# Two gate projections of a hybrid mixer as seven products of quarters

## The chip, the cores and the metric

The kernel runs on one core of a Trainium2 chip. It has five engines that work side by side, each through its own instructions in order: TensorE (PE; its weight loads are shown as PEld), VectorE (DVE), ScalarE (ACT), GpSimd (POOL) and SyncE (SP), which mostly issues DMAs. The metric is the device time of one execution in microseconds. A run of the kernel is compared with runs of the kernel before; smaller is better.

## What is computed

One decoder layer on 512 tokens of width 1024, in float32: a SwiGLU FFN, a mixer of two recurrent head groups, and a second FFN, each inside its own pair of norms.

```python
x = x + 0.5 * rms_norm(swiglu_ffn(rms_norm(x, norm_pre[0]), ffn1_w_in, ffn1_w_out), norm_post[0])
mixed = token_mixer(rms_norm(x, norm_pre[1]), w_mix_in, conv_w, ..., w_mix_out)
x = x + rms_norm(mixed, norm_post[1])
x = x + 0.5 * rms_norm(swiglu_ffn(rms_norm(x, norm_pre[2]), ffn2_w_in, ffn2_w_out), norm_post[2])
```

The mixer projects the normed x by one matrix and cuts the result into parts. The change concerns two of them, `hgate` (HG) and `mo` (MO), of 512 columns each:

```python
hq, hf, hi, hgate, mq, mk, mv, mo, mig, mfg = split_cols(h @ w_in, SPLIT_SIZES)
...
hg_o = rms_norm(hgrn2_chunkwise(...), hg_norm) * silu(hgate)
ml_o = rms_norm(mlstm_chunkwise(...), ml_norm) * sigmoid(mo)
return concatenate([hg_o, ml_o]) @ w_out
```

## The kernel before

**Number format.** Every float32 operand of a projection is split in a high part (`hi`, rounded to fp32r) and a low part (`lo = raw - hi`). A product takes three matmuls: high by high, high by low, low by high (`mm3`, lines L187, L188, L189). For a weight, ScalarE makes the high part and VectorE the low part (`split`, L283 and L285; for `w_mix_out`, whose rows are also scaled, L288 and L291 in halves of 512). The activations are split the same way into four tiles `xq`, one for each quarter of x (256 tokens by 512 columns): `to_t` transposes on TensorE (L353), then ScalarE casts (L359) and VectorE subtracts (L360).

**Stages.** FFN 1, the mixer, FFN 2. In the FFNs most projections are already made by seven products of quarters in place of eight (matmuls of 128x256 at L608, L947 and L955). The weight sums that the second projection of an FFN needs are made in DRAM: `sums_ahead` copies quarters of the weight to a DRAM tile by three DMAs of SP and adds others to it by three accumulating DMAs of GpSimd (L887). `make_sums` issues the next DMA of up to a few of these groups; it is called at places in the program (`EVERY`, the jobs of the mixer). FFN 1 has 13 such groups, FFN 2 has 15; the copies of seven of FFN 2's groups are issued at the end of FFN 1 (`copies_early`).

**The mixer.** The program is written in one order by hand; a scheduler at build time then orders each engine's instructions and may move one ahead of others whose operands it expects later (`behind` and `issue_after` pin some). Projections are generators (`job_f`, `job_t`); the recurrences call `fill(n)` between their steps, and each call runs the front job up to its next yield, so that projections fill TensorE while VectorE, ScalarE and GpSimd work on the recurrence. `job_t` makes 512 columns for all tokens in four PSUM banks: 4 weight tiles of 256 rows, 4 token tiles, 2 halves, 3 matmuls of 128x512 each, which is 96 matmuls. The last jobs are HG and MO; HG's result goes through Silu into the left half of `y`, MO's through Sigmoid and a multiplication on VectorE (L1771) into the right half (`gate_mo`).

Around them stand, in this order: `mlstm_scores`, four steps of `mlstm_values` (on VectorE L1679 to L1690, on GpSimd L344 and L1687), four steps of `hgrn_values` (VectorE L1651, GpSimd L345, VectorE L1657), the rest of MO, the transposes of `y` (L353), and the output projection `mix_out0`/`mix_out1`, whose first half needs `y`'s high and low parts (L359, L360).

**Loads.** All weights come through one ring of SBUF tiles (`raw`) by DMAs of SP; a load is issued behind the split of an earlier item (`load_due`). x itself (`xs`, 512 x 1024) stays in SBUF from the first norm to the output.

Of the kernel before, what the change touches and what calls it, by code (L numbers as in the profile page):

```python
# [14 lines left out]
P = 128  # L15
# [15 lines left out]
HQ, HF, HI, HG, MQ, MV, MO, MG = 0, 512, 1024, 1536, 2048, 2560, 3072, 3584  # L31
LEVELS = (1, 64, 32, 16, 8, 4, 2)
# [57 lines left out]
EVERY, EARLY, AHEAD = 5, 7, 13  # L90
# [28 lines left out]
class Layer:  # L119
    def __init__(self, ctx, tc, aps):  # L120
# [12 lines left out]
        self.xs = self.cp.tile([P, NT, D], F32, name="xs")  # L133
# [12 lines left out]
        }  # L146

# [112 lines left out]
    def split(self):  # L260
# [7 lines left out]
        else:  # L268
# [4 lines left out]
            n, o = self.lie("out" if it.key[1] == "out" else "mix" if it.key[0] == "mix" and b == 512 else "any")  # L273
# [20 lines left out]
        with self.behind(*self.hold):  # L294
            for out, other in it.adds:
                o, c = self.raw[out], self.raw[other]

                late = out[1] >= (HEAD if out[0] == "f1" else 1)
                added = (nc.vector if late else nc.gpsimd).tensor_tensor(o, o, c, op=ALU.add)  # L299
                if not late:  # L300
                    self.pooled = added
# [155 lines left out]
    def root(self, i, turned=False):  # L457

        x = self.xs[:, i, :]
# [8 lines left out]
    def scaled(self, i, g, r, xn, h):  # L468
        v = slice(512 * h, 512 * h + 512)
        scaled = self.nc.vector.scalar_tensor_tensor(xn[:, v], self.xs[:, i, v], r, g[:, v], op0=ALU.mult, op1=ALU.mult)  # L470
# [12 lines left out]
    def post1(self, i, y, parts, rms, pieces, g, out=None):  # L483
# [11 lines left out]
        for h, v in (late, (0, y)) if turned else ((0, y), late):  # L495
            x = self.xs[:, i, 512 * h : 512 * h + 512]
# [79 lines left out]
    def open_ffn(self, ctx, second=False):  # L576

        self.after_next, self.c22 = None, []
        self.second, self.filled = second, FILLED2 if second else FILLED
        hp = self.hpool = ctx.enter_context(self.tc.tile_pool(name=self.nm("hp"), bufs=1))  # L580
# [207 lines left out]
    def ffn_in(self):  # L788

        nc = self.nc  # L790
        if not self.second:
            self.begun = ()
            self.sums_due("f1")
        for n, (p, t) in enumerate(ORDER2[len(HEADS2) :] if self.second else ORDER[len(HEADS) :]):
            if n > 14 and n % EVERY == 0 and not self.second:
                self.make_sums()
            if n == 14 and self.second:

                with self.behind(self.pooled):
# [75 lines left out]
    def sums_ahead(self, f, h, k2, early=False):  # L875

        nc, to = self.nc, self.sums_of[f, h, k2]
        w, last = (self.ffn1_w_out, self.ffn2_w_out)[f == "f2"][0], self.loaded1 if early else self.loaded
        q = w[k2 * 2 * P : (k2 + 1) * 2 * P, h * 512 : (h + 1) * 512].rearrange("(k p) (c f) -> p k c f", p=P, f=QUARTER)
        with self.behind(last):  # L880
            nc.sync.dma_start(to[:, 0], q[:, 0, 1])
            nc.sync.dma_start(to[:, 1], q[:, 1, 0])
            nc.sync.dma_start(to[:, 2:], q[:, 1])
        yield
        for a, b, v in ((0, 2, q[:, 0, :1].broadcast_to([P, 2, QUARTER])), (2, 3, to[:, :1]), (3, 4, to[:, 2:3])):
            with self.behind(*([self.selected] if f == "f2" else [])):
# [3 lines left out]
    def sums_due(self, f, n=None, done=0):  # L890
        self.ahead, self.making = deque([k for k in self.sums_of if k[0] == f][done:n]), []

    def copies_early(self):

        self.begun = deque(self.sums_ahead(*k, early=True) for k in [k for k in self.sums_of if k[0] == "f2"][:EARLY])
# [3 lines left out]
    def make_sums(self):  # L899

        n = min(3, len(self.begun))
# [5 lines left out]
    def ffn_out(self, gpost_row, scale, after, trans, head):  # L907
# [89 lines left out]
        if self.second:  # L997
            self.sums_due("f2", done=AHEAD)
        n = 0
        for half in range(2):  # L1000
            C = [[self.ps() for _ in range(2)] for _ in range(2)]
            M, T, left = None, None, len(QF[half])
            for m, k2 in enumerate(OF[half][: PAIRS - LF * half]):
# [20 lines left out]
                if half == 0 and n % 2:  # L1024
# [14 lines left out]
        if not self.second:  # L1039
            self.copies_early()  # L1040
# [54 lines left out]
    def job_t(self, name, then):  # L1095

        acc = [self.ps() for _ in range(NT)]
        for k2 in range(ND // 2):
            w = self.pull()
            if name in ("hi", "mv"):  # L1100
                self.make_sums()
            for i in range(NT):
# [10 lines left out]
                yield  # L1113

    def mix_items(self):
# [17 lines left out]
        f(HF), f(HQ), f(MQ), t(HI), t(MV), t(HG), t(MO)  # L1133
# [66 lines left out]
    def small_params(self):  # L1200
# [29 lines left out]
        for g in range(2):  # L1230
            nc.sync.dma_start(self.gb[32 * g : 32 * g + 4, :], bias[g].rearrange("(h o) -> h o", o=1))
# [292 lines left out]
    def conv(self, n, ps):  # L1524
# [3 lines left out]
        nc.scalar.copy(x, ps)  # L1528
        tap = lambda j: self.prm[:, 4 * j + n : 4 * j + n + 1]
# [177 lines left out]
    def mixer(self):  # L1707
        nc, tc = self.nc, self.tc
        self.got, self.jobs = set(), deque()
        self.sums_due("f2", AHEAD, EARLY)  # L1710
        with tc.tile_pool(name="ma", bufs=1) as ma:
# [7 lines left out]
            self.eend = ma.tile([P, 16], F32, name="eend")  # L1719
            with tc.tile_pool(name="mb", bufs=1) as mb:  # L1720
# [30 lines left out]
            with tc.tile_pool(name="mc", bufs=1) as mc:  # L1751
                self.y = mc.tile([P, NT, D], F32, name="y")
                self.jobs.append(self.job_t("hg", lambda i, ps: nc.scalar.activation(self.y[:, i, :W], ps, AF.Silu)))
# [147 lines left out]
```

## Time and profile before

| | us |
|---|---|
| median of three runs | 934.02 (931.58 to 934.08) |
| the profiled execution | 933.69 |
| its span in the profile | 932.0 |
| TensorE busy | 921.7 (99%) |
| VectorE busy | 765.9 (82%) |
| ScalarE busy | 525.2 (56%) |
| GpSimd busy | 186.9 (20%) |

The span runs from the first to the last instruction that the profiler shows; 1.7 us of the profiled time lie around it. Busy time is the sum over an engine's instructions, overlaps counted once. In rows of the timeline the numbers are start and duration; x4 is the count of instructions in the row, and what stands in brackets is the idle time of the engine before it and what released it. In the chain of waits the duration of a matmul is its spacing in the stream, while the timeline and the groups show it from issue to end, so that neighbours overlap. FFN 1 ends and the mixer begins between about 320 and 347 us; the mixer ends at about 600 us.

### The profile page before, as it was taken

What the parts mean: (1) busy time and instruction counts of PE and PEld (TensorE: products, weight loads), DVE (VectorE), ACT (ScalarE), POOL (GpSimd) and SP (SyncE); (2) the same over time, 40 slices, a digit from 0 to 9 for tenths busy, and PEclk for the clock granted to TensorE, in tenths of its full rate; (3) what the DMA queues carried; (4) which work ended last, traced back from release to release, by engine and by line L of the source; (5) the groups of instructions that cost most, each with busy time, mean ns of one, the idle gap of its engine ahead of it and who ended that gap; (6) DMA issues with size and microseconds to landing.
All of it is one profiled execution on the core that took longest, in us unless ns stands there. A gap on an engine that the chain in (4) does not pass through costs nothing.

```text
span 932.0 us, 18308 instructions
## 1 busy us (share of the span) xinstructions
PE 921.7 (99%) x7423; PEld 887.4 (95%) x7423; DVE 765.9 (82%) x992; ACT 525.2 (56%) x757; POOL 186.9 (20%) x256
## 2 busy tenths in 40 slices
PE   8999999999999999999999999999999999999997
PEld 7999999999999999998887888899999999999997
DVE  5899978889888776698847564799898989998886
ACT  6645455557565466956633444495454545756661
POOL 3531112121111045452321210304000000011002
PEclk9999999999999999999999999999999999999999
DMA  9245679776797925798742124452453435279542
GB/s 310 76 138 157 181 182 214 195 157 142 209 273 238 262 65 150 151 184 208 152 98 69 46 72 132 137 162 66 135 159 123 136 111 174 84 221 261 165 153 91
DMA packets 118766, 145.42 MB, mean 156 GB/s; under 512 B 7413, under 2 KB 91417, under 8 KB 118682
## 3 DMA queue, kind: packets, MB, share of 16 engines
q1 hardware_dynamic: 102714, 129.05, 44.2%
q0 software_dynamic: 15680, 14.69, 11.6%
q8 instruction: 58, 0.95, 0.4%
q10 hardware_dynamic: 288, 0.52, 0.2%
q14 instruction: 26, 0.21, 0.1%
HBM read 142.14 MB, written 31.46 MB: 186 GB/s over the span
## 4 chain that ended last, share of the span: by engine, by line
PE 62%; ACT 1%; DVE 0%; issue 0%; POOL 0%; DVEq 0%; POOLq 0%; ACTq 0%
PE ps L608 22%; PE ps L955 8%; PE ps L538 6%; PE ps L187 5%; PE ps L189 5%; PE ps L188 5%; PE ps L947 4%; PE ps L1373 2%; PE ps L353 1%; PE ps L548 1%; PE ps L1466 0%; PE ps L1671 0%; PE ps L1644 0%; PE ps L1419 0%; PE ps L1668 0%; PE ps L1431 0%
## 5 line engine op out<-in xcount | busy, mean ns | idle before, releaser
L283 ACT CAST w<-raw 128x1024 fp32r<-128x1024 f32 x246 | 251.3, 1028 | 199.0 <-PE ps L608 93.6
L285 DVE TENSOR_TENSOR w<-raw,w 128x1024 fp32r<-128x1024 f32 x246 | 298.9, 1219 | 30.9 <-ACT w L283 29.5
L608 PE MATMUL ps<-xq,w 128*128 128x256 f32 x2016 | 237.1, 277 | 0.0
L608 PEld LDWEIGHTS ps<-xq,w 128*128 128x128 f32 x2016 | 232.9, 188 | 0.0
L608 PE MATMUL ps<-sq,w 128*128 128x256 f32 x1512 | 178.0, 276 | 0.3
L608 PEld LDWEIGHTS ps<-sq,w 128*128 128x128 f32 x1512 | 174.2, 188 | 1.0 <-ACT ps L659 0.9
L299 DVE TENSOR_TENSOR raw<-raw,raw 128x1024 f32<-128x1024 f32 x72 | 89.8, 1251 | 7.8 <-DMA raw<-in_ffn_w_in_dram 6.1
L955 PE MATMUL ps<-w,hs 128*128 128x256 f32 x672 | 81.0, 276 | 0.0
L947 PE MATMUL ps<-w,hs 128*128 128x256 f32 x672 | 79.2, 276 | 0.0
L955 PEld LDWEIGHTS ps<-w,hs 128*128 128x128 f32 x672 | 78.4, 188 | 0.0
L187 PE MATMUL ps<-w,xq 128*128 128x512 f32 x192 | 77.9, 407 | 0.1
L947 PEld LDWEIGHTS ps<-w,hs 128*128 128x128 f32 x672 | 77.5, 188 | 0.0
L189 PE MATMUL ps<-w,xq 128*128 128x512 f32 x192 | 74.8, 391 | 0.0
L188 PE MATMUL ps<-w,xq 128*128 128x512 f32 x192 | 74.8, 390 | 0.0
L538 PE MATMUL ps<-xq,w 128*128 128x256 f32 x480 | 57.5, 282 | 0.0
L538 PEld LDWEIGHTS ps<-xq,w 128*128 128x128 f32 x480 | 56.6, 189 | 0.5 <-issue 0.5
L887 POOL DMA_DIRECT2D f2sums<-in_ffn_w_out_dram x15 | 20.0, 1482 | 176.9 <-DMA f2sums<-in_ffn_w_out_dram 176.9
L827 ACT CAST hs<-hf 128x1024 fp32r<-128x1024 f32 x32 | 33.7, 1053 | 28.8 <-PE ps L955 21.1
L828 DVE TENSOR_TENSOR hs<-hf,hs 128x1024 fp32r<-128x1024 f32 x32 | 39.1, 1221 | 8.7 <-ACT hs L827 8.2
L887 POOL DMA_DIRECT2D f1sums<-f1sums x26 | 23.2, 892 | 105.9 <-DMA f1sums<-in_ffn_w_out_dram 53.0
L187 PEld LDWEIGHTS ps<-w,xq 128*128 128x128 f32 x192 | 36.1, 188 | 8.5 <-issue 1.0
L189 PEld LDWEIGHTS ps<-w,xq 128*128 128x128 f32 x192 | 36.1, 188 | 8.1 <-DVE xq L360 0.3
(262 smaller groups left out, 1223.3 us busy)
## 6 DMA issues: line engine op xcount, KB each, us to landing
raw<-in_ffn_w_in_dram SPq DMA_DIRECT2D x98, 512.0 KB, 5.3
raw<-in_ffn_w_out_dram SPq DMA_DIRECT2D x44, 512.0 KB, 4.5
raw<-in_w_mix_in_dram SPq DMA_DIRECT2D x28, 512.0 KB, 3.6
raw<-f2sums SPq DMA_DIRECT2D x15, 512.0 KB, 5.6
raw<-f1sums SPq DMA_DIRECT2D x13, 512.0 KB, 7.6
raw<-in_w_mix_out_dram SPq DMA_DIRECT2D x8, 512.0 KB, 3.7
f2sums<-in_ffn_w_out_dram SPq DMA_DIRECT2D x30, 128.0 KB, 5.9
f2sums<-in_ffn_w_out_dram SPq DMA_DIRECT2D x15, 256.0 KB, 5.7
```

Source lines behind the costliest of these rows:

```text
L187: mm(ps, sh, mh, start=start, stop=False, **kw)
L188: mm(ps, sh, ml, start=False, stop=False, **kw)
L189: mm(ps, sl, mh, start=False, stop=stop, **kw)
L283: nc.scalar.copy(hi, raw)
L285: self.low = nc.vector.tensor_tensor(lo, raw, hi.bitcast(F32), op=ALU.subtract)
L299: added = (nc.vector if late else nc.gpsimd).tensor_tensor(o, o, c, op=ALU.add)
L538: mm(ps[:, u0:u1], w[:, a, k, :], self.xop(k, b, u0, u1), start=k + n + m == 0, stop=k == ND - 1 and n == 2, skip_group_check=True,)
L608: self.nc.tensor.matmul(ps[:, c], wb[b][:, k, v], left[d][:, k, :], start=first and a + n + k == 0, stop=n == 2 and k == KH - 1, skip_grou ...
L828: self.nc.vector.tensor_tensor(lo, src, hi.bitcast(F32), op=ALU.subtract)
L887: nc.gpsimd.dma_start(to[:, a:b], v, accum_op=ALU.add)
L947: mm(out, a[kk][:, i * P : (i + 1) * P], w[:, b, kk, QUARTER * v : QUARTER * (v + 1)], start=begin and c == kk == n == 0, stop=kk == 1 and ...
L955: mm(ps[:, QUARTER * c : QUARTER * (c + 1)], A[a][:, c], B[b], start=begin and c == n == 0, stop=n == 2, skip_group_check=True,)
```

## The change

HG and MO are made by a new job, `job_unit`, from seven products of quarters (`UNIT`), each of 24 matmuls of 128x256 into half of the columns and half of the rows of a 512x512 result. x is cut into four quarters (256 tokens by 512 columns) and each gate's weight too (512 rows by 256 columns). Three of the seven weights are plain quarters, four are sums, made in DRAM with the machinery of FFN 1 (`unit_sums`: eight more groups behind the 13 of FFN 1, of which the first eight have their copies issued early). Four of the seven x operands are sums of quarters. For them the kernel writes x to DRAM at the start of the mixer (`spill`), makes the sums in x's place by eight operations of VectorE (`x_sums`), splits them in high and low parts (`sum_parts`), and loads x again at the end of the mixer.

The results of the products are combined by VectorE, three operations in each gate. One PSUM bank is held from the last convolution to the end of MO for one of the combined products. The gain tiles hold the high parts of two sums for a while, so their loads for this stage are issued later.

```diff
-EVERY, EARLY, AHEAD = 5, 7, 13
+EVERY, EARLY, AHEAD = 4, {"f1": 8, "f2": 7}, 13
...
-            self.begun = ()
-            self.sums_due("f1")
+            self.copies_early("f1", self.biased)
+            self.sums_due(("f1", "mix"), done=EARLY["f1"])
...
-                if half == 0 and n % 2:
+                if n % 2 if half == 0 else 0 < m < 5 and not self.second:
                     self.make_sums()
...
+            for _ in range({"hi": k2 // 2, "mv": 2}.get(name, 0)):
+                self.extra.popleft()()
...
+    def x_sums(self):
+
+        a, b, c, d = raws = [self.cp.tile([P, D], F32, tag=f"xs{n}", bufs=1, name=f"xsum{n}") for n in range(4)]
+        tt = lambda out, x, y, op: self.extra.append(lambda: self.nc.vector.tensor_tensor(out, x, y, op=op))
+        flat = lambda v: v.rearrange("p k t -> p (k t)")
+        whole = lambda out, q: tt(out, *(flat(v).bitcast(F32) for v in self.both(self.xq[q])), ALU.add)
+        whole(a, 0)
+        whole(b, 2)
+        tt(c, b, a, ALU.subtract)
+        whole(d, 3)
+        tt(b, b, d, ALU.subtract)
+        self.extra.append(lambda: self.sum_parts("p7"))
+        tt(a, a, b, ALU.subtract)
+        whole(d, 1)
+        tt(d, d, a, ALU.subtract)
+        self.extra.append(lambda: self.sum_parts("p5"))
...
+    def job_unit(self, name, put, keep):
+
+        if name == "hg":
+            self.sum_parts("p6", "p3")
+        nc, bank = self.nc, {"b6": self.whole}
...
+        into = {"p2": "p1", "p4": "p5", "p6": "b6", "p3": "b6"}
+        for p in UNIT:
+            w, x = self.pull(), self.unit_x[p]
+            if p not in into:
+                bank[p] = self.ps()
+            ps, n = bank[into.get(p, p)], 0
+            for a, b in ((0, 0), (0, 1), (1, 0)):
+                for c in range(2):
+                    for k in range(KH):
+                        nc.tensor.matmul(
+                            ps[:, QUARTER * c : QUARTER * (c + 1)], x[a][:, k, P * c : P * (c + 1)], w[:, b, k, :],
+                            start=p not in into and n == 0, stop=(a, k) == (1, KH - 1), skip_group_check=True,
+                        )
+                        n += 1
+                        if n % 6 == 0 and n < 24:
+                            yield
+            self.drop(w)
+            if p == "p1":
+                first = keep(1, 0)
+                nc.scalar.copy(first, two(ps))
+            elif p == "p5":
+                tt(two(bank["b6"]), two(ps), first, ALU.subtract)
+            elif p == "p2":
+                put(0, 0, two(ps))
+            elif p == "p6":
+                rest = keep(1, 1)
+                nc.scalar.copy(rest, two(ps))
+                tt(rest, two(bank["p7"]), rest, ALU.add)
+            elif p == "p4":
+                last = keep(1, 0, two(ps))
+                tt(last, two(ps), rest, ALU.subtract)
+                put(1, 1, rest)
+                put(1, 0, last)
+            elif p == "p3":
+                put(0, 1, two(ps))
+                self.got.add(name)
+            yield
...
+            for i in range(NT):
+                nc.sync.dma_start(self.spill[i], self.xs[i])
+            self.x_sums()
...
-                self.jobs.append(self.job_t("hg", lambda i, ps: nc.scalar.activation(self.y[:, i, :W], ps, AF.Silu)))
+                at = lambda n: slice(QUARTER * n, QUARTER * (n + 1))
+                self.jobs.append(self.job_kept("hg", lambda u, v: self.y[:, 2 * u : 2 * u + 2, at(v)], AF.Silu))
...
-                self.jobs.append(self.job_t("mo", self.gate_mo))
+                self.jobs.append(self.job_unit("mo", self.gate_mo, self.keep_mo))
...
                 for i in range(NT):
                     self.to_t(i, self.y[:, i], (0,))
+                self.new_x()
+                for i in range(NT):
+                    nc.sync.dma_start(self.xs[i], self.spill[i])
                 self.mix_out0()
```

114 lines of the change are left out of this document (82 added, 32 removed).

## The prediction

> **What bounds the kernel now.** I read the busy shares first, then windows cut at the stages around the change, then the chain of waits, then the timeline of VectorE at the two ends of the mixer.
>
> ```profile
> span 932.0 us, 18308 instructions
> PE 921.7 (99%) x7423; PEld 887.4 (95%) x7423; DVE 765.9 (82%) x992; ACT 525.2 (56%) x757; POOL 186.9 (20%) x256
> ...
> 60.00:320.00 260.00, 260.00 (x2292) 260.00 (x2292) 230.36 (x263) 146.87 (x190) 38.96 (x47) 1.00 0.77 203
> ...
> 345.00:400.00 55.00, 54.90 (x465) 54.22 (x464) 38.52 (x56) 43.25 (x51) 31.76 (x47) 1.00 0.68 160
> 400.00:480.00 80.00, 80.00 (x554) 72.19 (x553) 64.19 (x90) 44.22 (x59) 27.47 (x30) 1.00 0.82 172
> 480.00:515.00 35.00, 35.00 (x196) 28.02 (x196) 23.80 (x54) 11.88 (x21) 4.97 (x5) 1.00 0.22 64
> 515.00:553.00 38.00, 37.93 (x209) 32.77 (x208) 23.36 (x71) 16.24 (x27) 10.91 (x20) 1.00 0.21 69
> ```
>
> The columns of the windows are length, then busy time of PE, weight load, VectorE, ScalarE and GpSimd, then clock, DMA share and GB/s. TensorE never rests from 60 to 553 us, at full clock. So the program order of TensorE sets the time, and a removed matmul pays its spacing, unless another engine becomes late instead. VectorE is busy for 23.4 of the last 38 us of the mixer, but there it works in a serial chain, so its share alone doesn't say how much room it has.
>
> **What the products save.** These rows price one matmul: the 512-wide form from the first and the last of 40 consecutive ones in the mixer, the 256-wide form from the chain of FFN 2.
>
> ```profile
> 543.75 0.39 PE L189 MATMUL ps<-w,xq 128*128 128x512 f32 x1
> ...
> 552.59 0.39 PE L189 MATMUL ps<-w,xq 128*128 128x512 f32 x1
> ```
> ```profile
> 818.78 2.72 PE ps L608 x24
> 821.50 5.44 PE ps L947 x48
> ```
>
> Spacing of the wide form: (552.59 - 543.75)/39 = 0.2267 us. Of the narrow form: 2.72/24 = 0.1133 us. Half the columns cost half, so seven products of quarters keep their full arithmetic saving. Each gate has 96 wide matmuls now and 7 x 24 = 168 narrow ones then. For both: 192 x 0.2267 = 43.5 us against 336 x 0.1133 = 38.1 us, a saving of 5.4 us.
>
> The Trainium skill, "TensorE: Matmul & The Clock Gate", section "Back-to-back issue gap", speaks against the change: it gives sustained spacings of about 81 ns at 128 columns and 131 ns at 512 for streams of weight load and matmul, so that narrow ones would be dear. By its figures, as an estimate, 192 x 0.131 = 25 us would stand against at least 336 x 0.081 = 27 us, a loss. The rows above, 227 and 113 ns, disagree with it for these operands, and they decide.
>
> **Where the saving falls.** The two gates are filler between the steps of the recurrences. By the order of the instructions, the 192 wide matmuls of before stand as 72 up to the first mLSTM value step, 54 up to the last HGRN value step and 66 in one block behind it; the 336 narrow ones as 144, 108 and 84. The first two shares cost the same time (72 x 0.2267 = 144 x 0.1133 = 16.3 us, and 12.2 us each). The whole saving lies in the last block: 15.0 us become 9.5 us. Here stands what that block now covers.
>
> ```profile
> 538.01 0.23 PE ps L187
> 552.99 1.75 PE ps L353 x16
> ```
> ```profile
> 515.35 0.68 DVE L1680 TENSOR_REDUCE col<-sq 128x4 f32<-128x512 f32 x1
> ...
> 518.63 0.75 DVE L1690 TENSOR_TENSOR y<-ps,col 128x256 f32<-128x256 f32 x2 [1.74 <-POOL col L1687]
> ...
> 531.38 1.21 DVE L285 TENSOR_TENSOR w<-raw,w 128x1024 fp32r<-128x1024 f32 x1
> 532.51 0.68 DVE L1651 TENSOR_REDUCE col<-sq 128x4 f32<-128x512 f32 x1
> 534.60 1.13 DVE L1657 SCALAR_TENSOR_TENSOR y<-ps,col,y 128x128 f32<-128x128 f32 x4 [1.41 <-POOL col L345]
> ...
> 545.07 1.12 DVE L1657 SCALAR_TENSOR_TENSOR y<-ps,col,y 128x128 f32<-128x128 f32 x4 [1.41 <-POOL col L345]
> 546.11 2.98 DVE L291 SCALAR_TENSOR_TENSOR w<-raw,prm,w 128x512 fp32r<-128x512 f32 x4
> 550.25 1.38 DVE L1771 TENSOR_TENSOR y<-y,mo 128x512 f32<-128x512 f32 x2 [1.16 <-ACT mo L1769]
> ...
> 553.10 0.75 DVE L291 SCALAR_TENSOR_TENSOR w<-raw,prm,w 128x512 fp32r<-128x512 f32 x1
> 553.77 0.68 DVE L1771 TENSOR_TENSOR y<-y,mo 128x512 f32<-128x512 f32 x1
> 554.37 1.88 DVE L360 TENSOR_TENSOR xq<-ps,xq 128x512 fp32r<-128x512 f32 x3
> ```
>
> TensorE's transposes of y (L353) wait for the last HGRN value step, whose VectorE part ends at 546.11; before, they came 6.9 us after it, because the block was long. Behind them the first low half of y (L360, 554.37) lets mix_out go on. With the block at 9.5 us TensorE is at the transposes by 547.5, 5.4 us earlier, but VectorE has its own list to get through before L360, and it is in order. So I sum that list.
>
> **VectorE up to the first L360.** Up to the last HGRN step, the order of the changed kernel adds work at places where VectorE isn't waiting: one combining operation of the products ahead of the first HGRN reduction, and one half split of an output weight within the last step. The combining operation has this form:
>
> ```profile
> L627 DVE TENSOR_TENSOR ps<-ps,hf 128x512 f32<-128x512 f32 x37 | 25.7, 694 | 13.7 <-PE ps L608 13.7
> ```
>
> Its spacing when queued is that of L1771 above (554.37 - 553.77 = 0.60 us), the half split's 553.77 - 553.10 = 0.67. Further weight splits that are added fall into the waits on GpSimd shown in brackets (1.74 and 1.41 us, against 1.13 for a split, 532.51 - 531.38), or replace half splits that stood there; they cost nothing, and 1.1 us each if that cover is gone. So the last HGRN step ends 1.3 us later, at 547.4. Behind it the order lists, ahead of the first L360: four gate multiplications (as before), two combining operations, six half splits: 4 x 0.60 + 2 x 0.60 + 6 x 0.67 = 7.6 us. First L360 at 555.0, against 554.37: 0.6 us later. TensorE's 5.4 us turn into a wait there of about 6 us. Bounds: at best the serial chain gives back 1.3 us (none of it exposed), first L360 at 553.7, 0.7 us earlier; at worst two of the covered splits come out as well, 2.3 us later than in the sum. Behind L360 nothing differs but four loads of x and two of gains, which are needed only at the scaling and the addition after mix_out's first half.
>
> **The start of the mixer.** VectorE now also makes eight sums of 128x1024 from the normed x. The program has them beside the projections HI and MV, but in the order of the built kernel they stand at the mixer's start: one ahead of the weight split of 342.20, six behind the last L360 of x, one a little later.
>
> ```profile
> L299 DVE TENSOR_TENSOR raw<-raw,raw 128x1024 f32<-128x1024 f32 x72 | 89.8, 1251 | 7.8 <-DMA raw<-in_ffn_w_in_dram 6.1
> ```
> ```profile
> 342.20 1.23 DVE L285 TENSOR_TENSOR w<-raw,w 128x1024 fp32r<-128x1024 f32 x1
> ...
> 345.88 1.22 DVE L285 TENSOR_TENSOR w<-raw,w 128x1024 fp32r<-128x1024 f32 x1
> ...
> 359.59 1.24 DVE L285 TENSOR_TENSOR w<-raw,w 128x1024 fp32r<-128x1024 f32 x1 [4.96 <-ACT w L283]
> ```
> ```profile
> 345.88 1.23 DVE w L285
> 347.15 1.21 PE ps L548 x8
> ```
>
> TensorE waits at 347.15 for the split of 345.88, and VectorE runs without a gap from 342.20 to there. One sum in front of that costs its spacing, some 1.15 us, and TensorE has no later idle time to win it back. Six of the others fall into the 4.96 us of idle time ahead of 359.59, where they need 7.3 us; the weight split there slips by about 2.4 us. I take this as covered by the weights already split. Bounds: 0 us (the spill or the order lets the split go first) and 1.15 + 2.4 = 3.6 us. I take 1.15, the row next to it.
>
> **DRAM sums, spill, other engines.** Eight more groups of sums go through SP's and GpSimd's queues in FFN 1.
>
> ```profile
> q0 software_dynamic: 15680, 14.69, 11.6%
> raw<-f1sums SPq DMA_DIRECT2D x13, 512.0 KB, 7.6
> raw<-in_w_mix_out_dram SPq DMA_DIRECT2D x8, 512.0 KB, 3.7
> L1746 ACT ACT_TABLE_LOAD x4 | 5.1, 1283 | 0.1
> ```
>
> q0 carried 28 groups of 0.52 MB in 11.6% of 932 us, 3.9 us of all DMA engines each; eight more are 31 us in a stretch of 260 us with a share of 0.77, which makes 0.89. The copies on q1 come on top, 0.5 MB a group. But TensorE did not miss one microsecond in this window, and the row of L299 has 6.1 us of waiting for weights in the whole run, all of it covered: nothing, with 2 us as the upper bound (a third of those 6.1 us come out uncovered). The spill (four writes of 512 KB) is the cost of five landings of this kind at most and waits for nobody but the sums. Six more splits and two more function tables (1.28 us each) go to ScalarE, which has 16.2 busy us of 38 in the last window.
>
> The sum, on the profiled run: 933.69 - 5.4 (products) + 1.15 (start) + 6.0 (wait before mix_out) = 935.4, which is 1.75 = 1.15 + 0.6 us over before. The median of the runs shown is 0.33 us above the profiled one, so I say 935.6 us.
>
> **The rivals.** A: the tail isn't the bound, since VectorE catches up in the shorter waits or the order on the chip lets L360 go early. TensorE then keeps all of it: 933.69 - 5.4 + 1.15 = 929.4. For it speaks that TensorE is at 99% and sets the whole chain now; against it the list of 7.6 us, which no longer has a block of 15 us beside it. B, on the other side: the fourth output weight comes late. Its load stands in SP's queue behind reloads of x and of the gains, and needs the buffer that the first output weight's split frees, at 547.4 + 1.15 + 0.6 + 0.67 = 549.8. With 3.7 us to landing it is there at 553.5, and its high half (0.7 us on ScalarE) at 554.2. VectorE reaches its low half, which stands 1.3 us ahead of the first L360, at 556.15 - 1.3 = 554.9 (555.0 of the sum above, with the start's 1.15). So there is 0.7 us of room: a landing over 4.4 us decides, and the 7.6 us of the loads of sums cost 3.9 - 0.7 = 3.2 us more, 938.8, with the 2 us of FFN 1 on top 940.8. For it speak 2.5 MB of reloads that stand in the same stretch, against it the DMA share of 0.21. C: the change doesn't work as filler, the products wait for their sums from DRAM or for x's quarters; a wait of one landing of 7.6 us would give 943. The groups are made 100 us ahead, so this is unlikely.
>
> **How the numbers follow.** A difference under 0.3% (2.8 us) can't be told from none here. Forecast 0.58, whose own range is 932.5 to 938 (the bounds of the two ends of the mixer, taken singly); A 0.19; B 0.18; C 0.05. Below 931.2 lie A and little else: 0.18. Over 936.8 lie B, C and the upper part of the forecast's range (0.15): 0.38. Within: 0.44. The range reaches into A and through B: 930 to 940.
>
> **What would show it.** Right: L608's spacing of 0.113 us in the products; a first mixer matmul about 1 us late; TensorE idle for 5 to 7 us just ahead of mix_out, released by VectorE's L360 of the new kernel or by the cast before it; the last HGRN step within 1 us of its old distance to the first mLSTM step. Wrong: no such idle time (A), idle time released by a load of w_mix_out (B), gaps within the products (C), or gaps in 60 to 320 us, where I put none.

## The result, and the profile after

The changed kernel takes 936.52 us (median of 17 runs, 934.14 to 939.5), the kernel before 931.58 us in the runs beside them (929.57 to 934.08, 17 runs). The ratio is 1.0055, with a 95% interval of 1.0045 to 1.0064: slower, by some 5 us. The forecast of 935.6 us was made against a profile of before that ran 2 us above the median; the change it forecast was 1.75 us.

This is the head of the page and the two windows around the mixer's end, of the changed kernel (columns as in the prediction), and then its waits of TensorE (us in total, times, longest):

```profile
span 933.4 us, 18752 instructions
PE 919.5 (99%) x7567; PEld 892.1 (96%) x7567; DVE 789.1 (85%) x1016; ACT 537.7 (58%) x773; POOL 215.3 (23%) x280
...
515.00:553.00 38.00, 35.31 (x276) 34.38 (x275) 25.87 (x71) 16.44 (x28) 12.33 (x20) 0.96 0.45 139
553.00:620.00 67.00, 64.88 (x369) 55.39 (x368) 44.73 (x63) 39.37 (x78) 10.43 (x25) 1.00 0.47 148
```
```profile
PE ps L1181 <- ACT mo L1198: 2.4, 1, 2.4
PE ps L193 <- ACT xq L365: 1.9, 1, 1.9
...
PE ps L554 <- DVE w L291: 0.8, 1, 0.8
```

TensorE has less to do (919.5 us busy against 921.7) and rests where it never did: 0.8 us at the mixer's start, 2.4 us within MO's products (L1181), 1.9 us ahead of mix_out (L193). The clock is 0.96 in the window of the mixer's end, where before it was 1.00 throughout.

VectorE has the reason. This is its timeline in the changed kernel, from the list ahead of the first mLSTM step to the first low part of y (L366):

```profile
505.06 0.61 DVE L1749 COPY C<-ps 64x129 f32<-64x129 f32 x2 [1.23 <-PE ps L1739]
...
509.71 0.69 DVE L1170 TENSOR_TENSOR y<-ps,y 128x512 f32<-128x512 f32 x1
...
512.95 0.69 DVE L1170 TENSOR_TENSOR y<-ps,y 128x512 f32<-128x512 f32 x1
513.56 1.21 DVE L291 TENSOR_TENSOR w<-raw,w 128x1024 fp32r<-128x1024 f32 x1
...
514.83 0.67 DVE L1798 TENSOR_REDUCE col<-sq 128x4 f32<-128x512 f32 x1
...
518.84 0.68 DVE L1798 TENSOR_REDUCE col<-sq 128x4 f32<-128x512 f32 x1
...
520.34 1.23 DVE L291 TENSOR_TENSOR w<-raw,w 128x1024 fp32r<-128x1024 f32 x1
523.03 0.76 DVE L1808 TENSOR_TENSOR y<-ps,col 128x256 f32<-128x256 f32 x2 [1.47 <-POOL col L1805]
...
534.31 0.68 DVE L1769 TENSOR_REDUCE col<-sq 128x4 f32<-128x512 f32 x1
...
548.08 0.61 DVE L1775 SCALAR_TENSOR_TENSOR y<-ps,col,y 128x128 f32<-128x128 f32 x2
548.60 0.68 DVE L1898 TENSOR_TENSOR y<-y,ps 128x512 f32<-128x512 f32 x1
...
555.57 0.68 DVE L1898 TENSOR_TENSOR y<-y,ps 128x512 f32<-128x512 f32 x1
556.17 2.48 DVE L366 TENSOR_TENSOR xq<-ps,xq 128x512 fp32r<-128x512 f32 x4
```

The list behind the last HGRN step is as forecast: 556.17 - 548.60 = 7.6 us without a gap. But what stands in front of it is later than forecast. In the mLSTM step from 518.84 the split at 520.34 was to be hidden by the wait on GpSimd; the wait behind it is still 1.47 us, and the step to L1808 takes 4.2 us. GpSimd's rows in the two kernels show why. First the kernel before (first profile), in an mLSTM step without a split and in the HGRN step that has a half split at 536.23; then the changed one, in an mLSTM step without a split and in one with a split:

```profile
521.07 0.20 POOL L344 TENSOR_SCALAR col<-col 128x4 f32<-128x4 f32 x1 [2.48 <-DVE col L1685]
...
536.40 0.62 POOL L344 TENSOR_SCALAR col<-col 128x4 f32<-128x4 f32 x1 [1.84 <-DVE col L1651]
```
```profile
516.47 0.19 POOL L350 TENSOR_SCALAR col<-col 128x4 f32<-128x4 f32 x1 [21.70 <-DVE col L1803]
...
520.48 1.14 POOL L350 TENSOR_SCALAR col<-col 128x4 f32<-128x4 f32 x1 [2.41 <-DVE col L1803]
```

The same instruction on four columns takes 0.19 us, 0.62 us beside a half split, and 1.14 us where a whole split runs beside it: GpSimd ends with the split, not beside it. The Trainium skill, "GPSIMD Engine Reference", section "Key points", has GpSimd's SBUF interfaces shared with VectorE, with contention where VectorE has two inputs in SBUF or runs in a 2-port mode; the split has two inputs in SBUF, and the rows agree.

The products have not the price of the forecast either. This is the one long piece of them in the chain of waits of the changed kernel, and then TensorE's timeline of the last block in the two kernels where that block has no wait in it: 84 narrow matmuls in `kept_warm_9` (an experiment below, with the same products), 66 wide ones in the second profile of before:

```profile
493.23 4.34 PE ps L1181 x36
```
```profile
537.37 3.60 PE L1192 MATMUL ps<-w,xq 128*128 128x256 f32 x28
540.80 1.12 PE L1192 MATMUL ps<-w,xpart 128*128 128x256 f32 x8
541.76 5.12 PE L1192 MATMUL ps<-w,xq 128*128 128x256 f32 x40
546.72 1.12 PE L1192 MATMUL ps<-w,xpart 128*128 128x256 f32 x8
547.68 2.28 PE L363 MATMUL ps<-ident,y 128*128 128x128 f32 x16
```
```profile
534.12 0.48 PE L187 MATMUL ps<-w,xq 128*128 128x512 f32 x1
...
549.17 1.91 PE L353 MATMUL ps<-ident,y 128*128 128x128 f32 x16
```

The spacing is 4.34/36 = 0.1206 us, not 0.1133, and the block of 84 (28 + 8 + 40 + 8 in the rows) takes 547.68 - 537.37 = 10.3 us against 549.17 - 534.12 = 15.05: it saves 4.7 us and not 5.5. The other shares don't break even, as the forecast had them, but cost: summed from the starts of TensorE's instructions, the first 144 narrow matmuls take 18.25 us where 72 wide ones took 17.73, the next 108 take 14.0 where 54 took 13.0. In all 42.6 us against 45.8: TensorE saves some 3.2 us.

### The profile page after: what moved, and what is told of

It reads as the page before. It is cut to its first block, busy times and chain, and to the rows that moved or that the text cites. A ratio compares the mean times of both kernels' runs of the same rounds, so it can differ in the third digit from the quotient of the medians.

```text
span 933.4 us, 18752 instructions
## 1 busy us (share of the span) xinstructions
PE 919.5 (99%) x7567; PEld 892.1 (96%) x7567; DVE 789.1 (85%) x1016; ACT 537.7 (58%) x773; POOL 215.3 (23%) x280
## 4 chain that ended last, share of the span: by engine, by line
PE 56%; DVE 3%; issue 2%; POOL 1%; ACT 1%; DVEq 0%; POOLq 0%; ACTq 0%
PE ps L615 22%; PE ps L970 8%; PE ps L544 6%; PE ps L962 4%; PE ps L193 3%; PE ps L195 3%; PE ps L194 3%; PE ps L1490 2%; PE ps L1181 2%; PE ps L554 1%; POOL col L351 1%; DVE w L291 1%; PE ps L359 1%; ACT w L294 0%; PE ps L1583 0%
## 5 line engine op out<-in xcount | busy, mean ns | idle before, releaser
L289 ACT CAST w<-raw 128x1024 fp32r<-128x1024 f32 x252 | 257.6, 1028 | 179.3 <-PE ps L615 91.4
L291 DVE TENSOR_TENSOR w<-raw,w 128x1024 fp32r<-128x1024 f32 x252 | 306.3, 1220 | 18.8 <-ACT w L289 17.7
L193 PE MATMUL ps<-w,xq 128*128 128x512 f32 x128 | 51.2, 403 | 2.0 <-ACT xq L365 1.9
L194 PE MATMUL ps<-w,xq 128*128 128x512 f32 x128 | 49.9, 391 | 0.0
L195 PE MATMUL ps<-w,xq 128*128 128x512 f32 x128 | 49.6, 391 | 0.1
L902 POOL DMA_DIRECT2D f2sums<-f2sums x30 | 25.2, 879 | 87.2 <-DMA f2sums<-in_ffn_w_out_dram 50.5
L305 POOL TENSOR_TENSOR raw<-raw,raw 128x1024 f32<-128x1024 f32 x12 | 31.6, 2640 | 41.0 <-DVE w L291 39.6
L448 ACT ACTIVATE junk<-ps 128x256 f32<-128x256 f32 (+1 forms) x40 | 17.1, 428 | 40.7 <-DVE ps L927 20.1
```

The source lines that it names most:

```text
L193: mm(ps, sh, mh, start=start, stop=False, **kw)
L194: mm(ps, sh, ml, start=False, stop=False, **kw)
L195: mm(ps, sl, mh, start=False, stop=stop, **kw)
L289: nc.scalar.copy(hi, raw)
L291: self.low = nc.vector.tensor_tensor(lo, raw, hi.bitcast(F32), op=ALU.subtract)
L902: nc.gpsimd.dma_start(to[:, a:b], v, accum_op=ALU.add)
```

## The experiments

Each kernel was timed in turn with the kernel before on one chip. To compare profiles, I cut each at eight marks: the first FFN matmul of 128x256, the first matmul of the mixer, the first of the 288 matmuls of the forget and query projections, VectorE's first reduction of the mLSTM steps, its first of the HGRN steps, the end of its last HGRN step, the first low part of y, and the first 24 matmuls of FFN 2. The second profile of before (`before_again`) and that of the changed kernel give, for example, these rows of the chain of waits (the first mixer matmul of the changed kernel is not on its chain; the timeline has it at 341.05):

```profile
340.45 6.12 PE ps L548 x48
...
353.88 32.64 PE ps L538 x288
...
599.35 2.82 PE ps L608 x24
```
```profile
355.65 32.64 PE ps L544 x288
...
604.33 2.82 PE ps L615 x24
```

Differences to `before_again`, in us (its own lengths in the first line):

| | FFN 1 | mixer's start | to mLSTM | mLSTM steps | HGRN steps | list | to FFN 2 | sum |
|---|---|---|---|---|---|---|---|---|
| before_again | 328.16 | 13.43 | 157.84 | 17.14 | 13.68 | 8.18 | 48.63 | 587.06 |
| changed kernel | +0.28 | +1.17 | +1.34 | +2.34 | +0.70 | -0.70 | -0.47 | +4.66 |
| all_but_products | +0.48 | +1.16 | 0.00 | +0.01 | 0.00 | 0.00 | 0.00 | +1.65 |
| two_lows_out | 0.00 | +1.17 | +1.35 | +0.61 | +0.69 | -0.69 | +0.96 | +4.09 |
| late_gates | +0.20 | +1.19 | +1.34 | +2.35 | +1.36 | -4.02 | +1.49 | +3.91 |
| hg_only | 0.00 | 0.00 | +1.34 | +1.00 | -0.01 | -2.92 | -0.07 | -0.66 |

**before_again.** 

> The kernel before once more, for a second profile: whether the 288 matmuls of the forget and query projections at the mixer's start take 33.9 us again, as in the first profile, or 32.6, as in every profile of the other kernels, and whether VectorE's first reduction of the mLSTM steps comes at 515.35 - 1.8 then.

931.29 us in this one run. The 288 matmuls take 32.64 us, as in the changed kernel; the 33.92 us of the first profile are an accident of that run (two other kernels show it too), and the first reduction comes at 511.72. So the first profile had 1.3 us of slow matmuls in a place where no edit was made. It is 1.7 us longer between the first and the last mark, and comparing with it alone would have shown the change too cheap by as much.

**all_but_products.**

```diff
-        for u, c0 in enumerate(UNITS):
-            unit(u, c0)
+        t(HG), t(MO)
...
-                self.jobs.append(self.job_unit("mo", self.gate_mo, self.keep_mo))
+                self.jobs.append(self.job_t("mo", self.gate_mo))
```

> The changed kernel with the gates' products as before (96 matmuls of 512 columns each), but with everything around them: the weight sums in DRAM, the spill, the eight sums of x, the split of two of them, the reload; the sums are not used. Theory 1: the last block is 15 us long again and covers VectorE's list, so the time is that of before plus what the start of the mixer costs, 0 to 1.2 us: ratio 1.000 to 1.0015. Theory 2: most of the 5 us stays, 1.003 to 1.005.

933.07 us, ratio 1.0026 (1.0016 to 1.0037): between the kernel before and the changed one, and above the 1.0015 of theory 1. The table tells where: 1.16 us at the mixer's start, 0.48 us in FFN 1, and nothing behind them. The spill, the seven other sums of x and the reload cost nothing that this profile shows; the end of the mixer is that of before to 0.01 us. The 0.48 us are the subject of the next run.

**no_dram_sums.**

```diff
-EVERY, EARLY, AHEAD = 4, {"f1": 8, "f2": 7}, 13
+EVERY, EARLY, AHEAD = 5, {"f1": 8, "f2": 7}, 13
...
-            self.copies_early("f1", self.biased)
-            self.sums_due(("f1", "mix"), done=EARLY["f1"])
+            self.begun = ()
+            self.sums_due(("f1",))
...
-                if p in ("p1", "p2", "p3"):
-                    k, c = int(p != "p1"), int(p == "p3")
+                if True:
+                    k, c = int(p in ("p2", "p3", "p6")), int(p in ("p3", "p4", "p7"))
```

> The changed kernel with plain quarters of the weight in place of the four sums (so the gates come out wrong), and with FFN 1's DMAs as in the kernel before; products, sums of x, spill and reload stay. Theory 1: as the changed kernel, 1.005 (1.004 to 1.006). Theory 2, for its half on FFN 1's transfers: 1.000 to 1.003.

934.99 us, ratio 1.0042 (1.0028 to 1.0055). The interval overlaps that of the changed kernel, so the time alone leaves anything from nothing to some 3 us for FFN 1's added transfers. The profiles say more. FFN 1 takes 328.16 us here, as in before_again, and 328.16 to 328.19 in every other profile without the added groups or with four of them (hg_only). In the eight profiles with all eight groups it takes 0 to 1.98 us more, 0.6 on average. The changed kernel has 0.28 us of this and no wait that the profile lists. In seven of the eight, VectorE waits 0.3 to 3.0 us for a load of FFN 1's weights at about 90 us; without added groups no profile has such a wait there. kept_warm_9 (below) has the most of both; VectorE works without a gap from there, and TensorE waits for it and ScalarE at 102 and 108 us:

```profile
91.36 1.23 DVE L309 TENSOR_TENSOR raw<-raw,raw 128x1024 f32<-128x1024 f32 x1 [3.01 <-DMA raw<-in_ffn_w_in_dram]
```

So the added transfers do cost time, a small and varying amount. The wait and the lost time don't go together in every profile (all_but_products loses 0.48 us without it), so the late load need not be all of it.

**two_lows_out.**

```diff
+LEFT = [("mix", n) for n in (30, 31)]
...
-            self.low = nc.vector.tensor_tensor(lo, raw, hi.bitcast(F32), op=ALU.subtract)
+            if it.key not in LEFT:
+                self.low = nc.vector.tensor_tensor(lo, raw, hi.bitcast(F32), op=ALU.subtract)
```

> The changed kernel without the low parts of two weights of MO (its fourth and fifth product), the two splits of VectorE that stand in the waits of the mLSTM steps; those products use stale low parts. Theory 1a (a split with two operands in SBUF holds GpSimd up, whose first operation in the step took 1.14 us in place of 0.19 there): the steps with a split shrink from 5.0 and 4.7 us to 4.0, the first low part of y comes 1.9 us earlier, ratio 1.003. Theory 1b (the splits are hidden in those waits, as the prediction had it): no change, 1.005. Theory 2 (start of the mixer, transfers): no change either, 1.005, but the steps would tell: they shrink under 1a alone.

936.44 us, ratio 1.0053 (1.0041 to 1.0066). The steps shrink as 1a has it, by 2.34 - 0.61 = 1.73 us, with GpSimd's operation back at 0.20 us, and the first low part comes earlier by as much. Yet the time is that of the changed kernel: 1.4 us are given back between the low part and FFN 2 (+0.96 against -0.47). Something behind the low part takes them; late_gates shows it plainly.

**late_gates.**

```diff
+                copied = nc.scalar.copy(rest, two(ps))
+                if name == "mo":
+                    with self.behind(copied):
+                        put(0, 0, two(bank["p1"]))
...
+                with self.behind(self.low):
+                    for y, g in self.gated:
+                        nc.vector.tensor_tensor(y, y, g, op=ALU.mult)
```

> The changed kernel, with three things moved at the end of the mixer and nothing left out: MO's copy of the sixth product goes ahead of the output weights' high halves and the first sigmoid on ScalarE; the four gate multiplications and the low halves of the third and fourth output weight go behind the low parts of y on VectorE. Theory 1 (VectorE's list between the last HGRN step and the first low part of y sets the end): of the list's 7.6 us remain two combining operations and two to four half splits, 2.5 us (3.2 with one more half split ahead of the last step). The first low part comes 4.4 us earlier than in the changed kernel's profile (556.2), TensorE no longer waits 2.4 us for the copy, and the time is some 4 us below the changed kernel, ratio to before 1.001 (0.999 to 1.003). Theory 2 (the start of the mixer or FFN 1's added transfers cost the time): as the changed kernel, 1.005.

936.2 us, ratio 1.005 (1.0036 to 1.0063): no gain, against the forecast of theory 1. The wait within the products is gone, and the list is 3.3 us shorter than in the changed kernel (-4.02 against -0.70), where the expectation had 4.4 to 5.1; VectorE now waits for the first cast, which came only at 552.57 on ScalarE. But look at TensorE right behind its wait, in the timeline and in windows of 5 us:

```profile
553.21 0.50 PE L194 MATMUL ps<-w,xq 128*128 128x512 f32 x1 [3.46 <-ACT xq L368]
553.54 0.40 PE L195 MATMUL ps<-w,xq 128*128 128x512 f32 x1
553.93 0.63 PE L196 MATMUL ps<-w,xq 128*128 128x512 f32 x1
...
557.35 0.49 PE L195 MATMUL ps<-w,xq 128*128 128x512 f32 x1
```
```profile
550.00:555.00 5.00, 1.79 (x5) 1.17 (x6) 3.56 (x7) 4.53 (x9) 0.00 (x0) 0.91 0.64 188
555.00:560.00 5.00, 5.00 (x18) 3.98 (x18) 5.00 (x10) 0.85 (x2) 0.00 (x0) 0.74 0.60 209
```

For 3.4 us each matmul takes 0.43 us in place of 0.23, and the granted clock of the window is 0.74. So this idle time of TensorE costs twice: while it lasts, and some 1.6 us behind it (eight matmuls at 0.43 - 0.23). In the changed kernel the wait of 2.4 us within MO's products is followed by such a stretch too: the last 24 matmuls of 128x256 took 551.57 - 547.33 = 4.2 us in place of the 2.9 that 24 x 0.1206 make (551.57 is the start of the transposes behind them). There it was hidden, since TensorE had to wait for VectorE again anyway. In two_lows_out TensorE waits 3.3 us ahead of mix_out, and the clock of its window from 555 to 560 us is 0.70: the slow stretch lies behind the low part and is no longer hidden. That fits the 1.4 us given back there, and the 1.49 here.

Not every wait of this length is followed by such a stretch. The second wait of the changed kernel, 1.85 us ahead of mix_out, is not, nor is one of 1.99 us in the same place of first_sum_later (below), whose window shows it:

```profile
555.00:560.00 5.00, 4.86 (x20) 3.64 (x21) 3.74 (x7) 2.17 (x5) 0.00 (x0) 1.00 0.65 229
```

In both a slow stretch had ended shortly before. What decides it, beyond the length of the wait, no run shows.

**gates_behind_casts**, late_gates with three sigmoids and one weight's high half behind the casts of y, and the first sum of x behind the first weight splits:

```diff
+                self.taken = [self.cast]
+                for y, g, src in self.gated[1:]:
+                    with self.behind(self.cast):
+                        nc.scalar.activation(g, src, AF.Sigmoid)
...
+            def one():
+                with self.behind(first):
+                    self.nc.vector.tensor_tensor(out, x, y, op=op)
```

> As late_gates, with two more moves and nothing left out: three of MO's four sigmoids and the high half of the third output weight go behind the casts of y on ScalarE, and the first sum of x behind the mixer's first weight splits on VectorE. Theory 1: in late_gates the first cast waited for ScalarE until 552.6; now it comes right behind the transposes at 549.6 to 550, TensorE idles about 1 us in place of 3.5 and keeps its clock (the slow stretch of 3.4 us had cost 1.6 us), and the mixer's start is 1.2 us earlier: 3.5 to 5.5 us below late_gates, ratio 0.999 to 1.001. Theory 2 (the idle time isn't what costs, something in common with everything but the products is): 1.003 to 1.005.

932.73 us, ratio 1.0012 (1.0 to 1.0024), 3.5 us below late_gates, at the edge of what theory 1 had. The first cast comes at 549.33, right behind the transposes. TensorE still waits 1.9 us, now for the first low part behind VectorE's list, and the slow stretch comes back, as its window shows:

```profile
555.00:560.00 5.00, 5.00 (x18) 3.96 (x17) 5.00 (x9) 0.73 (x2) 0.00 (x0) 0.74 0.81 281
```

**gates_kept_warm and kept_warm_9** fill that wait with idle matmuls:

```diff
+                            for _ in range(IDLE):
+                                mm(acc[1][:, :P], self.ident, self.ident, start=True, stop=True)
```

> gates_behind_casts with 18 idle matmuls of 128x128 (their results are overwritten) in the place where TensorE waited 1.9 us for the first low part of y; nothing left out. Theory 1c (the low clock of some 3.4 us behind such a wait, eight matmuls of 0.43 us in place of 0.23, is the answer to the idle time): the clock stays at 1.00 between 550 and 560 us, the eight matmuls take 0.23 us each, and the time is 1.3 to 1.7 us below gates_behind_casts, ratio 0.9990 to 1.0005. Theory 1d (the matmuls are slow since their operands come late or SBUF is busy with reloads): the same spacing of 0.43 us with the idle matmuls, no change, 1.001.

> gates_kept_warm with 9 idle matmuls in place of 18, since 18 took 4.0 us (36 records of 0.11 us) where TensorE had 1.9 us to wait: they kept the clock at 1.00, but held the third matmul up until 553.5, 2 us after its operand. Theory 1c (the low clock answers the idle time): 9 take 2.0 us, the clock stays at 1.00, and the time is 1.5 to 2 us below gates_kept_warm and 1 to 1.6 us below gates_behind_casts: ratio 0.9995 to 1.0015. Theory 1d (the clock isn't it): no better than gates_behind_casts, 1.0012 or more, with the low clock back.

With 18: 934.0 us, 1.0033 (1.0021 to 1.0046), slower than without them, where a gain was expected. The clock stayed at 1.00, but they ran 2 us longer than the wait. With 9: 930.87 us, ratio 0.9996 (0.9987 to 1.0005). That is 1.5 us below gates_behind_casts by the ratios, whose intervals overlap a little; and the profiles agree: from the first low part to FFN 2 it takes 50.15 us in gates_behind_casts and 48.66 in kept_warm_9 (48.63 in before_again). The step from 18 to 9 paid 3.4 us by the ratios, more than the 1.5 to 2 expected. Here is the window of the low clock in kept_warm_9:

```profile
550.00:555.00 5.00, 5.00 (x30) 4.41 (x31) 5.00 (x9) 4.63 (x8) 0.00 (x0) 1.00 0.67 168
555.00:560.00 5.00, 5.00 (x23) 4.13 (x22) 4.41 (x7) 0.00 (x0) 0.00 (x0) 1.00 0.93 341
```

The clock is 1.00 with matmuls that compute nothing, under the same reloads (DMA share 0.93, against 0.81 in gates_behind_casts): it answers TensorE's idle time, not its operands or the reloads. The Trainium skill, "TensorE: Matmul & The Clock Gate", section "What's actually happening", has half the clock after an idle window of some 3.4 us, until a busy one of that length. The 3.4 us at half speed agree; but here waits of 1.9 and 2.4 us sufficed, though not each wait of about 1.9.

**probe_port**, the kernel before with three idle operations of VectorE in the mLSTM steps:

```diff
+                if c == 1:
+                    nc.vector.tensor_tensor(probe, vh[:, :D], vh[:, D:], op=ALU.add)
+                elif c == 2:
+                    nc.vector.tensor_copy(probe, vh[:, :D])
+                else:
+                    nc.vector.tensor_tensor(probe[:, :512], vh[:, :512], vh[:, D : D + 512], op=ALU.add)
```

> The kernel before with three idle operations of VectorE added in the waits of the mLSTM steps: in the second a sum of two tensors in SBUF of 128x1024, in the third a copy of 128x1024, in the fourth a sum of 128x512. Theory 1a (an operation with two operands in SBUF holds GpSimd): GpSimd's first operation in the second step takes some 1.1 us in place of 0.19, in the fourth some 0.5 or more; the copy tells whether operations with one operand do it as well (0.19 if not, 0.7 if so). Theory 1b (GpSimd runs beside them): 0.19 in all. The time of the whole stays within 0.3% under both, since the steps have 6.9 us to spare in the kernel before.

934.09 us in its one run, 0.3% above the median beside it; 1.3 us of that are the 288 matmuls, which took 33.92 us here. GpSimd's first operation in the four steps:

```profile
515.11 0.20 POOL L344 TENSOR_SCALAR col<-col 128x4 f32<-128x4 f32 x1 [21.22 <-DVE col L1685]
...
519.19 1.10 POOL L344 TENSOR_SCALAR col<-col 128x4 f32<-128x4 f32 x1 [2.47 <-DVE col L1685]
...
524.14 0.57 POOL L344 TENSOR_SCALAR col<-col 128x4 f32<-128x4 f32 x1 [2.47 <-DVE col L1685]
...
528.56 0.57 POOL L344 TENSOR_SCALAR col<-col 128x4 f32<-128x4 f32 x1 [2.47 <-DVE col L1685]
```

1a holds, and the copy with one operand in SBUF does it as well: in each of the three steps GpSimd's operation ends when VectorE's added one (1.22, 0.69 and 0.69 us) is over.

**first_sum_later**, the changed kernel with the pin of gates_behind_casts alone:

> The changed kernel with one thing moved: the first sum of x goes behind the mixer's first weight splits on VectorE (as in hg_only and gates_behind_casts). Theory 1 (that sum alone is the cost of the mixer's start, 1.45 to 1.6 us in the profiles, and all of what everything but the products costs): the forget and query projections begin at most 0.2 us later than in the kernel before, counted from the first matmul of FFN 1, TensorE's wait ahead of the mixer's first projection (0.8 us) is gone; the end of the mixer begins earlier by as much and stays as it is, so 1.2 to 1.6 us below the changed kernel, ratio 1.0035 to 1.0045. Rival (the mixer's end is set by VectorE's list, and what VectorE doesn't do at the start it does later): 1.005 to 1.006.

935.62 us, ratio 1.0048 (1.0029 to 1.0067). In the profile the mixer's start takes 13.45 us (355.06 - 341.61), against 14.60 in the changed kernel and 13.43 in before_again: the moved sum was the whole cost of the start. Nothing of it is given back before the first reduction: the stretch there is 159.19 us, as in the changed kernel. In the time, the interval is too wide to tell 1.0048 from 1.0055.

**hg_only.** With only HG by seven products and the same pin (parts of the diff are left out; p6 and p3 keep their operands in other tiles than in the changed kernel):

```diff
-UNITS = (HG, MO)
+UNITS = (HG,)
...
-                self.jobs.append(self.job_unit("mo", self.gate_mo, self.keep_mo))
+                self.jobs.append(self.job_t("mo", self.gate_mo))
```

> Only HG by seven products, MO as in the kernel before (so 2.7 us of TensorE saved in place of 5.4, four groups of weight sums in place of eight), and the first sum of x pinned behind the mixer's first weight splits. The parts of two sums lie in other places, since MO needs x whole. Nothing is left out. Theory 1 (VectorE's list ends last, and TensorE's idle time lowers its clock): VectorE has no combining operations of MO and three splits fewer behind the first mLSTM step, so the block of filler behind the last HGRN step, 12 us, still covers its list: no idle time of TensorE ahead of mix_out, clock 1.00 throughout, and 2 to 3 us below the kernel before, ratio 0.997 to 0.999. Theory 2 (what stands around the products, sums of x, spill and DMAs, costs the time): 1.002 or more, as with everything but the products.

929.78 us (12 runs), ratio 0.9982 (0.9971 to 0.9992): faster than both kernels, by 1.7 us against the kernel before. Its profile is 0.66 us shorter between the marks; the rest of the gain lies where nothing was changed, so 0.66 is what the profiles can account for. Its windows around the first low part (549.79):

```profile
545.00:550.00 5.00, 5.00 (x33) 4.36 (x32) 4.23 (x8) 4.07 (x9) 0.00 (x0) 1.00 0.64 209
550.00:555.00 5.00, 5.00 (x24) 3.88 (x23) 2.93 (x5) 1.61 (x4) 0.00 (x0) 1.00 0.15 34
```

TensorE has no idle time there and keeps its clock. In the table the list shrinks by 2.9 us: the steps end 2.3 us later than before and the transposes come 0.6 us earlier, and VectorE's list, without MO's combining operations, still fits between them. From the first of the 288 matmuls to the transposes of y TensorE needs 194.88 us against 195.46 in before_again, 0.58 us less. Half of the 3.2 us that two gates save is some 1.6; the rest goes for the most part into its one longer wait in the mLSTM steps, which come late here too (+1.34, +1.00):

```profile
525.53 1.13 PE L1777 MATMUL ps<-vh,sT 128*128 128x128 f32 x8 [1.10 <-DVE y L1823]
```

## Why the prediction came out as it did

The mechanism was right in the main: TensorE's saving falls in the last block, and VectorE's list behind the last HGRN step takes it back. The time lay in the stated range, but the change is 4.9 us where the sum had 1.75, and "no change" was the likeliest case where "slower" came. The marks say where the difference lies. To the forecast 1.75 come 1.73 (splits in the waits on GpSimd), 1.34 (up to the first mLSTM step) and 0.28 (FFN 1), all three put at nothing, and 0.47 us are won behind the first low part: 4.63, against 4.66 in the table. Of the signs that it named, the late start of the mixer came; the spacing of 0.113 us, 5 to 7 us of idle time just ahead of mix_out and the HGRN steps within 1 us of their old distance did not (0.1206; 1.9 us; 3.0 us later). By its steps:

- *Products, 5.4 us saved*: mis-sized. The price of 0.1133 us, taken from FFN 2, did not carry over: these products run at 0.1206 us, and the saving is 3.2 us. The 288 matmuls of the projections in the same mixer do run at 32.64/288 = 0.1133, so it is not the stage; the cause is open. Since VectorE's list, without a gap from 548.60 to 556.17, sets the end of the mixer, the time of the changed kernel should hang little on it; the wait just comes out shorter than the 6 us forecast.
- *Start of the mixer, 1.15 us*: right in place, cause and size: 1.17 us from the mixer's first matmul to the projections, and nothing of it left with that sum moved (first_sum_later). The bound of the six other sums (2.4 us) wasn't touched.
- *The list, 7.6 us*: right to 0.1 us, and so are the 1.3 us of work added up to the last HGRN step (0.61, what two_lows_out leaves of the mLSTM steps' delay, and 0.70 in the HGRN steps).
- *"They cost nothing" of the splits in the waits on GpSimd*: this step failed. Two splits cost 1.73 us together (two_lows_out), because GpSimd's operation ends only when they are over. The row that shows it was in the first profile, and the prediction did not read it: GpSimd's 0.62 us at 536.40, shown above. The prediction's own fallback of 1.1 us each was near.
- *Up to the first mLSTM step*: the sum had nothing, and it cost 1.34 us. Before, VectorE idled 2.2 us ahead of its last split there, as its timeline in before_again has it:

```profile
510.32 1.23 DVE L285 TENSOR_TENSOR w<-raw,w 128x1024 fp32r<-128x1024 f32 x1 [2.22 <-ACT w L283]
511.58 0.23 DVE L1679 COPY col<-ps 128x2 f32<-128x2 f32 x2
```

  In the changed kernel HG's two combining operations and its splits fill that time and more: from 505.06 to the first reduction VectorE's timeline has no gap. hg_only has the same 1.34 us, so it belongs to HG's product form. TensorE reaches the value matmuls of this step 0.5 us later as well, but that is not what the reduction waits for while VectorE's list has no gap. How much of the 1.34 us would stay with a shorter list was not tested.
- *The wait ahead of mix_out, "about 6 us"*: TensorE's idle time came in two parts, 2.4 us within MO and 1.9 us ahead of mix_out, with a slow stretch between them. Within MO, the copy of the sixth product stood behind weight halves, a function-table load of 1.28 us and a sigmoid on ScalarE. The prediction had set ScalarE's added work at nothing by its busy share of the window; as for VectorE, the share didn't tell what stands in line at one moment. It named gaps within the products as a sign of rival C, but this one has another cause. When mix_out can go on is set by VectorE's list and not by these waits.
- *DRAM sums and spill, nothing, up to 2 us*: the bound was right and the "nothing" was not quite: 0.28 us of FFN 1 in the changed kernel's profile, 0 to 1.98 in all eight with these groups.
- *Rival A* (the gain is kept) is refuted by the idle time. *B* (a late weight) didn't come: VectorE's list has no gap ahead of that weight's half split at 554.90. *C*: no product waited for its sums from DRAM.

One mistake was in the ground and not in a step: the profile of before ran 1.3 us slow in one stretch, and the median of three runs was 2.4 us above that of 17. That the forecast of 935.6 us came within 1 us of the measured 936.52 is luck: a base too high by 2.4 us and a change too small by 3.1 nearly cancel.

## What to carry to other kernels

When TensorE's filler is shortened beside a serial chain on another engine, find the block in which the saved time falls, and sum what the chain's engine must issue up to the next matmul; half of the saving with all of the cover beat all of the saving with none (hg_only at 0.9982 against first_sum_later at 1.0048, both with the first sum of x moved). A wait on GpSimd is no free slot for VectorE's operations: they hold the answer up until they are over. And an idle TensorE can cost more than its wait: look at the granted clock behind it, and either close the gap or fill it with matmuls of just its length.

## What the runs showed that I had not expected

I had not expected the low clock behind waits of 1.9 to 3.5 us, with matmuls at 0.43 us in place of 0.23 for some 3.4 us, nor that 9 idle matmuls undo it, nor that other waits of 1.85 and 1.99 us were not followed by it. Eight more groups of sums in FFN 1 cost nothing there in one profile and 2 us in another. The same form of matmul, 128x256 in float32 with 128x128 weights, takes 0.1133 us in the FFN and 0.1206 us in the gates' products; no run told why. And the 288 matmuls take 32.64 us in most profiles and 33.92 in three of them at a granted clock of 1.00; what causes that stays open.
